# A batched matmul kernel on one core: one more turn, jumped over, at the front of TensorE's loop

## The chip, the cores and the metric

The kernel runs on one core of one Trainium2 chip. A core has five engines that each run their own list of instructions and meet through semaphores: TensorE (PE, matmuls), VectorE (DVE), ScalarE (ACT), GpSimd (POOL) and SyncE (SP, which here issues transfers only). Sixteen DMA engines move data between the chip's memory (HBM) and the core's on-chip memory. The metric is the device time of one execution in microseconds (us); lower is better.

## The reference

```python
x, y: float32 of shape (8, 12, 512, 64)
out = np.einsum('bhtc,bhsc->bhts', x, y)      # float32 of shape (8, 12, 512, 512)
```

There are 96 heads; each is a product of a 512x64 matrix with the transpose of another 512x64 matrix. The inputs have 25.17 MB together, the output has 100.66 MB.

## The kernel before

**Tiles.** The 96 heads are taken in 6 groups of 16. A group's x or y is one transfer of 2 MB (`load`, line 165), so there are 12 loads. An output tile is 2 MB too, and there are 48 of them. Five buffers of 2 MB, the `slots`, hold whatever comes in from HBM or goes out to it; loads and output tiles take them in turn.

**Stages.** ACT, DVE and POOL narrow a loaded slot to bf16 (`compress`), put x in an order fit for a transposition (`mix`), and DVE transposes 32x32 blocks (`transposes`, lines 214 and 223). PE multiplies (line 255, and line 262 for two tiles in each turn whose rows are laid out so that one store of 4 MB covers two tiles), writing into one of two PSUM buffers `pm0` and `pm1`, each half a tile. ACT copies a finished half from PSUM into a slot (`result`, line 409). SP stores the slot (`store`, lines 396 and 400). One output tile, number 41 (`SPLIT`), is made in two ways: half of its rows go the normal way, the other half are computed in five pieces late in the run (`pieces`, line 338), and sent by SP and POOL in small transfers (`send`, lines 373 and 382); POOL also issues two tiny reads (`step`, line 360).

**Order.** The whole work lies in one critical section in which the program writes the semaphore waits itself. A helper, `emit`, adds an instruction to an engine, works out which counts it has to wait for, and notes the count that the instruction will raise. All engines but PE are written out straight. PE alone runs a loop (`all_products`): 6 turns, 8 output tiles in a turn. Its waits compare a semaphore with a register: the counter `t` takes the values 8, 16, ... 48, and `counts` holds t-7 to t. Before tile j it waits until `tr` (transposes finished) has reached its count, at j = 0 and 4, and before each half tile until `ev0` or `ev1` (halves copied out of PSUM, plus one at the start) has reached `counts[j]`. So that PE's first half tile need not wait, ACT raises `ev0` and `ev1` by one at the start (line 431). Inside the loop stand jumps: at j = 1 and j = 5 one that skips the five late pieces in all turns but the last (line 286), and at the end of a turn two for its last two tiles (line 293), which are done in the narrow way in the first and the last turn and in the wide way in the others.

**The end.** When the critical section is over on all engines, a last store of 2 MB goes out (line 478), and the run ends when it has landed.

Of the kernel before, what the change touches and what calls it, by code (L numbers as in the profile page):

```python
# [9 lines left out]
def kernel(  # L10
# [22 lines left out]
    nc = tc.nc  # L33
# [8 lines left out]
    V = G // 4  # L42
    K = 8
    E = R // K
    D = 32
    SLOTS = 5
    TURNS = NH // 2
    SPLIT = V * NH - 2 * V + 1
    GROUP = 4
# [16 lines left out]
    wide = out.rearrange("b h t s -> (b h t s)").rearrange(  # L66
        "(o u g q n) -> o g q u n", u=2, g=V // 2, q=Q * E, n=2 * K * S
    )
# [3 lines left out]
    ps = ctx.enter_context(tc.tile_pool(name="ps", bufs=1, space=bass.MemoryType.PSUM))  # L72
    slot_row = sb.tile([P, SLOTS * K * S], fp32, name="slots")
    slots = [slot_row[:, i * K * S:(i + 1) * K * S] for i in range(SLOTS)]
    keep = sb.tile([P, (NG - 1) * R * D + (2 * NG - 1) * R // 2 * D], u32, name="keep")
# [16 lines left out]
    sems, ticks, known, snaps, writer, readers = {}, {}, {e: {} for e in engines}, {}, {}, {}  # L92
# [23 lines left out]
    def emit(name, make, reads=(), writes=(), dma=None, lane=None, known_by=None, held=None):  # L116

        points = [writer[r] for r in (*reads, *writes) if r in writer]
        points += [v for w in writes for v in readers.get(w, ())]
        if name == "pool" and name in ticks:  # L120
            points.append((name, ticks[name]))
        need(name, points, known_by, held)
        p, step = (lane or name, V if lane == "tr" else 1) if dma is None else (f"dma{dma}", 16)
        if p not in sems:
            sems[p] = tc.alloc_semaphore(p)
        if held is not None:
            held.append(make)
        elif make is not None:
            make().then_inc(sems[p], step)
        at = (p, ticks.get(p, 0) + step)  # L130
        ticks[p] = at[1]
        snaps[at] = {**known[name], p: at[1]}
        if dma is None:
            for q in lanes.get(name, (name,)):
                snaps[at][q] = ticks.get(q, 0)
        for r in reads:
            readers.setdefault(r, []).append(at)
        for w in writes:
            writer[w], readers[w] = at, []
# [17 lines left out]
    def slot():  # L157
        made_slots.append((len(made_slots) + 1) % SLOTS)
        return made_slots[-1]

    def load(n):
        i = loaded[n] = slot()
        emit(
            "sp",
            lambda: nc.sync.dma_start(slots[i], (yv if n % 2 else xv)[n // 2]),  # L165
            writes=both(i),
            dma=i,
        )
# [74 lines left out]
    def products(o, k):  # L243
        i, half, pm = o // V, o // V % 2, k // 4
        emit("pe", None, [("xT", half), ("yT", half)] + [("x_wide",)] * ((i + 1) * V - 1 in WIDE), [("pm", pm)],
             known_by=[(f"ev{pm}", o + 1), ("tr", (i + 1) * V)])

    def four(j, pm, wide):
        half, h = divmod(j, V)
        xT = xTs[half].bitcast(bf16).rearrange("p (k h m) -> p k h m", k=K, h=V)  # L250
        yT = yTs[half].bitcast(bf16)
        xw = ybs[1][0].bitcast(bf16).rearrange("p (k h w m) -> p k h w m", k=K, h=2, w=2)
        for b in range(4):
            if not wide:
                last = nc.tensor.matmul(  # L255
                    pms[pm][:, b, :], xT[:, 4 * pm + b, h, :], yT[:, h * S:(h + 1) * S],
                    start=True, stop=True,
                )
                continue
            for i in range(2):  # L260
                at = V - 2 + i
                last = nc.tensor.matmul(  # L262
                    pms[pm][i * 64:(i + 1) * 64, b, :], xw[:, 4 * pm + b, i, j % 2, :],
                    yT[:, at * S:(at + 1) * S],
                    start=True, stop=True,
                )
        return last

    def all_products():

        with nc.tensor.Fori(2 * V, 2 * V * TURNS + 1, 2 * V) as t:
            counts = [nc.tensor.snap(t - i) for i in range(2 * V - 1, 0, -1)] + [t]

            def tile(j, wide=False):

                if j % V == 0:
                    nc.tensor.wait_ge(sems["tr"], counts[j + V - 1])
                for pm in range(2):
                    nc.tensor.wait_ge(sems[f"ev{pm}"], counts[j])
                    four(j, pm, wide).then_inc(sems["pe"], 1)  # L280

            for j in range(2 * V - 2):
                tile(j)
                for o in BEHIND:
                    if o % (2 * V) == j:
                        with nc.tensor.If(t == 2 * V * (o // (2 * V) + 1)):
                            for step in held[o]:
                                if callable(step):
                                    step().then_inc(sems["pe"], 1)
                                else:  # L290
                                    nc.tensor.wait_ge(sems[step[0]], step[1])
            for wide, turns in enumerate((t % (2 * V * (TURNS - 1)) == 2 * V, t % (2 * V * (TURNS - 1)) != 2 * V)):
                with nc.tensor.If(turns):
                    for j in range(2 * V - 2, 2 * V):
                        tile(j, bool(wide))
# [59 lines left out]
    def step(at):  # L355

        to = spare[0:17:4, :, at * D // 2:(at + 1) * D // 2]
        emit(
            "pool",
            lambda: nc.gpsimd.dma_start(to, xv[0, 0:5].rearrange("p (a b c) -> p a b c", a=2, c=D)[:, :, 0, :D // 2]),  # L360
            dma="side",
        )
# [39 lines left out]
    def result(o, s):  # L402

        for k in range(0, K, 4):
            pm = k // 4
            products(o, k)
            emit(
                "act",
                lambda: nc.scalar.activation(  # L409
                    slots[s][:, k * S:(k + 4) * S], pms[pm].rearrange("p j s -> p (j s)"), COPY  # L410
                ),
                [("pm", pm)],
                [("slot", s, pm)],
                lane=f"ev{pm}",
            )
        if o < V * NH - 1:
            store(o, s)

    def prepare(i):

        if i < NH:
            transposes(i)
        if i + 1 < NH:
            for part in range(4):
                mix(i + 1, "dve", part)

    with tc.tile_critical(sync_engine=mybir.EngineType.Pool) as work:  # L427
        for at in range(2):
            sems[f"ev{at}"] = tc.alloc_semaphore(f"ev{at}")
            ticks[f"ev{at}"] = 1  # L430
            nc.scalar.sem_inc(sems[f"ev{at}"], 1)
        for g in range(SLOTS):
            load(g)
        step(0)
        for half, name in enumerate(("dve", "pool")):
            emit(
                name,
                lambda: engines[name].memset(xbs[half], 0.0),  # L438
                writes=[("xb", half, part) for part in range(4)],
            )  # L440
        front = []
        for n in range(2 * NG):
            if n == 11:
                result(3, slot())
            compress(n)
            mix(n // 4, "pool", n % 4)
            if n == 4:
                transposes(0)
            if n < 5:
                load(n + SLOTS)  # L450
            elif n in (6, 8):
                load(n // 2 + 7)
            elif n < 10:
                front.append(slot())
            if n > 7 and n < 11:
                result(n - 8, front[n - 8])
            if n == 9:
                transposes(1)
        prepare(2)
        for o in range(V, V * NH):  # L460
            result(o, slot())
            if o in BEHIND:
                pieces(o)
            if o == max(BEHIND):
                send()
            if o % V == V - 1:
                prepare(o // V + 2)
            if o == SPLIT - V - 1:
                pick()
        all_products()  # L470
    with tc.tile_critical() as rest:
        need("dve", [(p, ticks[p]) for p in ("dmaside", *(f"dma{i}" for i in range(SLOTS)))])
    tc.add_manual_dep(
# [40 lines left out]
```

## Time and profile before

| what | value |
|---|---|
| time, median of 3 runs | 299.59 us (299.47 to 299.66) |
| the profiled execution's own time | 299.59 us |
| its span, first to last instruction | 297.8 us |
| mean granted TensorE clock | 0.812 |
| bytes moved | 125.87 MB, mean 423 GB/s |
| busy: ACT, DVE, PE, POOL | 213.9, 161.9, 138.2, 58.5 us |
| last store issued | 287.17 us after the span's start |

The profile shows one execution. The span leaves out 1.79 us around the first and the last instruction (299.59 - 297.8). "DMA" in the profile's strip of forty slices is the busy share of the sixteen DMA engines. A transfer of 2 MB is cut into 128 packets of 16,384 bytes, eight for each DMA engine, and every DMA engine raises the transfer's semaphore by one when its own eight are done; the trace keeps these sixteen times for each transfer, so it shows by how much the slowest of the sixteen is behind the others. Packets of kind "instruction" carry program code to an engine, over the same DMA engines.

### The profile page before, as it was taken

The numbers are of one execution on the slowest core, as the hardware profiler recorded it, in microseconds if no ns is written. First come the engines' busy times: TensorE is split into PE (matmuls) and PEld (weight loads), VectorE is DVE, ScalarE is ACT, GpSimd is POOL, SyncE is SP. The second block draws the span as 40 slices with busy tenths as digits, with TensorE's granted clock in tenths as the row PEclk, the third lists the DMA queues.
The fourth block names the chain that finished last, engine by engine and source line by source line (L and its number), as shares of the span: only waits on it lengthen the run. The fifth ranks groups of instructions, "written<-read, shape, count | busy, mean of one in ns | idle before, by whom it ended". The sixth has DMA issues, their size and how long they took to land.

```text
span 297.8 us, 1449 instructions
## 1 busy us (share of the span) xinstructions
PE 138.2 (46%) x466; PEld 38.4 (13%) x466; DVE 161.9 (54%) x85; ACT 213.9 (72%) x111; POOL 58.5 (20%) x27
## 2 busy tenths in 40 slices
PE   0000040457655655743765844555827656755500
PEld 0000010111111111110121111211102112211100
DVE  2167797899929692935808639168095344103000
ACT  1665666999999987681998647978549965496900
POOL 3399999992000000000000000000000000002000
PEclk9999999998799997695598575996557986599755
DMA  7999999999999999999999999999999999999997
GB/s 275 429 429 436 427 429 425 429 427 434 434 425 431 434 431 424 436 447 416 427 438 428 453 414 429 429 431 429 429 436 429 423 425 462 394 434 431 423 407 319
DMA packets 8219, 125.87 MB, mean 423 GB/s; under 512 B 1036, under 2 KB 1036, under 8 KB 1052
## 3 DMA queue, kind: packets, MB, share of 16 engines
q1 hardware_dynamic: 8056, 125.11, 98.7%
q0 software_dynamic: 160, 0.72, 0.6%
q8 instruction: 1, 0.02, 0.0%
q14 instruction: 2, 0.02, 0.0%
HBM read 25.17 MB, written 100.66 MB: 423 GB/s over the span
## 4 chain that ended last, share of the span: by engine, by line
DMA 52%; ACT 29%; PE 6%; issue 4%; DVE 3%; ACTq 1%; SPq 0%; POOLq 0%
DMA out_dram<-slots 38%; ACT slots L409 26%; DMA slots<-in_y_dram 7%; DMA slots<-in_x_dram 6%; PE pm L255 4%; ACT keep L147 3%; DVE keep L149 3%; PE pm L338 2%; ACTq L427 1%; SPq L165 0%; ACTq L109 0%; SPq L109 0%; SPq L509 0%; POOLq L427 0%; POOLq L498 0%
## 5 line engine op out<-in xcount | busy, mean ns | idle before, releaser
L409 ACT ACTIVATE slots<-pm 128x2048 f32<-128x2048 f32 x96 | 173.4, 1892 | 43.1 <-DMA out_dram<-slots 33.9
L255 PE MATMUL pm<-yT,xT 128*128 128x512 bf16 x320 | 113.0, 498 | 125.1 <-ACT slots L409 83.4
L214 DVE STREAM_TRANSPOSE xT<-xb 128x2048 uint32<-128x2048 uint32 x12 | 46.7, 3889 | 66.7 <-PE pm L255 32.8
L255 PEld LDWEIGHTS pm<-yT,xT 128*128 128x128 bf16 x320 | 30.0, 114 | 208.2 <-ACT slots L409 132.6
L147 ACT ACTIVATE keep<-slots 128x4096 bf16<-128x4096 f32 (+1 forms) x12 | 36.5, 3042 | 21.5 <-DMA slots<-in_x_dram 16.3
L149 DVE COPY xb<-keep 32x2048 bf16<-32x2048 bf16 x36 | 47.0, 1306 | 1.0
L149 DVE CAST keep<-slots 64x2048 bf16<-64x2048 f32 x12 | 36.2, 3018 | 17.1 <-DMA slots<-in_y_dram 16.9
L373 POOL DMA_DIRECT2D out_dram<-keep x2 | 1.1, 564 | 205.0 <-ACT keep L147 205.0
L149 POOL COPY xb<-keep 32x2048 bf16<-32x2048 bf16 x12 | 36.3, 3024 | 9.2 <-ACT keep L147 8.4
L262 PE MATMUL pm<-yT,keep 128*64 128x512 bf16 x128 | 18.4, 415 | 12.4 <-ACT slots L409 12.4
L223 DVE STREAM_TRANSPOSE yT<-keep 128x1024 uint32<-128x1024 uint32 x12 | 23.1, 1926 | 0.0
L149 DVE COPY keep<-pm 96x2048 f32<-96x2048 f32 x3 | 6.9, 2287 | 24.9 <-PE pm L338 24.9
L149 POOL CAST keep<-slots 64x2048 bf16<-64x2048 f32 x6 | 17.8, 2970 | 1.4 <-DMA slots<-in_y_dram 0.8
L262 PEld LDWEIGHTS pm<-yT,keep 128*64 128x64 bf16 x128 | 6.2, 114 | 24.3 <-ACT slots L409 20.5
L338 PE MATMUL pm<-yT,keep 128*96 128x512 bf16 x18 | 6.9, 515 | 4.1 <-ACT slots L409 4.1
L147 ACT ACTIVATE keep<-pm 96x2048 f32<-96x2048 f32 (+1 forms) x2 | 2.9, 1446 | 2.8 <-PE pm L338 2.8
L338 PEld LDWEIGHTS pm<-yT,keep 128*96 128x96 bf16 x18 | 2.3, 151 | 8.3 <-issue 3.6
L234 DVE COPY keep<-xT 128x1024 uint32<-128x1024 uint32 x4 | 2.7, 674 | 0.0
L438 DVE MEMSET xb<- 128x2048 uint32 x1 | 1.8, 1765 | 1.4 <-PEq L498 1.4
L147 ACT ACT_TABLE_LOAD x1 | 1.3, 1283 | 1.0 <-PEq L498 1.0
L438 POOL MEMSET xb<- 128x2048 uint32 x1 | 1.8, 1823 | 0.0
L360 POOL DMA_DIRECT2D spare<-in_x_dram x2 | 1.2, 618 | 1.2 <-POOLq L427 1.2
(6 smaller groups left out, 1.4 us busy)
## 6 DMA issues: line engine op xcount, KB each, us to landing
out_dram<-slots SPq DMA_DIRECT2D x39, 2048.0 KB, 17.1
out_dram<-slots SPq DMA_DIRECT2D x4, 4096.0 KB, 20.8
slots<-in_x_dram SPq DMA_DIRECT2D x6, 2048.0 KB, 18.6
slots<-in_y_dram SPq DMA_DIRECT2D x6, 2048.0 KB, 20.8
out_dram<-slots SPq DMA_DIRECT2D x1, 1024.0 KB, 18.3
out_dram<-keep POOLq DMA_DIRECT2D x2, 352.0 KB, 10.0
out_dram<-keep SPq DMA_DIRECT2D x2, 128.0 KB
out_dram<-keep SPq DMA_DIRECT2D x1, 64.0 KB
```

Source lines behind the costliest of these rows:

```text
L147: lambda: nc.scalar.activation(dst, src, COPY)
L149: else engines[name].tensor_copy(dst, src),
L214: lambda: nc.vector.transpose(xTs[half].rearrange("p (k r e) -> p k e r", k=K, e=E), xbs[half].rearrange("p (k e c) -> p k e c", k=K, e=E),),
L223: lambda: nc.vector.transpose(yTs[half].rearrange("p (r j) -> p j r", r=D), ybs[half][b].rearrange("p (j c) -> p j c", c=D),),
L234: lambda: nc.vector.tensor_copy(x_wide, xTs[1].rearrange("p (k h q w) -> p k h w q", k=K, h=V, w=2)[:, :, V - 2:],),
L255: last = nc.tensor.matmul(pms[pm][:, b, :], xT[:, 4 * pm + b, h, :], yT[:, h * S:(h + 1) * S], start=True, stop=True,)
L262: last = nc.tensor.matmul(pms[pm][i * 64:(i + 1) * 64, b, :], xw[:, 4 * pm + b, i, j % 2, :], yT[:, at * S:(at + 1) * S], start=True, stop ...
L338: last = nc.tensor.matmul(pms[pm][:96, b, :], picked[:, bank, :], yT[:, h * S:(h + 1) * S], start=True, stop=True,)
L360: lambda: nc.gpsimd.dma_start(to, xv[0, 0:5].rearrange("p (a b c) -> p a b c", a=2, c=D)[:, :, 0, :D // 2]),
L409: lambda: nc.scalar.activation(slots[s][:, k * S:(k + 4) * S], pms[pm].rearrange("p j s -> p (j s)"), COPY),
L427: with tc.tile_critical(sync_engine=mybir.EngineType.Pool) as work:
L438: lambda: engines[name].memset(xbs[half], 0.0),
```

## The change

The loop starts at `t` = 8 still, but runs to 56: seven turns. In the first of them, an `If(t > TURN)` around the whole body sends PE past it, so that PE goes from the loop's head to its foot and back. The other six turns do the same work as before, with `t` from 16 to 56. As the registers are 8 higher, the semaphores are too: ACT raises `ev0` and `ev1` by 9 in place of 1, and `tr` by 8, at the start. The tests that pick the last turn, and the first and last, are moved by one turn.

```diff
+    TURN = 2 * V
...
     def products(o, k):
...
-             known_by=[(f"ev{pm}", o + 1), ("tr", (i + 1) * V)])
+             known_by=[(f"ev{pm}", TURN + o + 1), ("tr", TURN + (i + 1) * V)])
...
-        with nc.tensor.Fori(2 * V, 2 * V * TURNS + 1, 2 * V) as t:
+        with nc.tensor.Fori(TURN, TURN * (TURNS + 1) + 1, TURN) as t, nc.tensor.If(t > TURN):
             counts = [nc.tensor.snap(t - i) for i in range(2 * V - 1, 0, -1)] + [t]
...
-                        with nc.tensor.If(t == 2 * V * (o // (2 * V) + 1)):
+                        with nc.tensor.If(t == TURN * (o // TURN + 2)):
...
-            for wide, turns in enumerate((t % (2 * V * (TURNS - 1)) == 2 * V, t % (2 * V * (TURNS - 1)) != 2 * V)):
+            for wide, turns in enumerate((t % (TURN * (TURNS - 1)) == 2 * TURN, t % (TURN * (TURNS - 1)) != 2 * TURN)):
...
-        for at in range(2):
-            sems[f"ev{at}"] = tc.alloc_semaphore(f"ev{at}")
-            ticks[f"ev{at}"] = 1
-            nc.scalar.sem_inc(sems[f"ev{at}"], 1)
+        for lane, count in (("ev0", TURN + 1), ("ev1", TURN + 1), ("tr", TURN)):
+            sems[lane] = tc.alloc_semaphore(lane)
+            ticks[lane] = count
+            nc.scalar.sem_inc(sems[lane], count)
```

`V` is 4 and `TURNS` is 6, so `TURN` is 8 and a loop turn makes 8 output tiles.

## The prediction

> **What bounds the kernel now.** I read the page first: the engines' busy time, the strip of forty slices, and the DMA queues.
>
> ```profile
> PE 138.2 (46%) x466; PEld 38.4 (13%) x466; DVE 161.9 (54%) x85; ACT 213.9 (72%) x111; POOL 58.5 (20%) x27
> ...
> DMA  7999999999999999999999999999999999999997
> ...
> q1 hardware_dynamic: 8056, 125.11, 98.7%
> q0 software_dynamic: 160, 0.72, 0.6%
> q8 instruction: 1, 0.02, 0.0%
> q14 instruction: 2, 0.02, 0.0%
> ```
>
> No engine is busy for more than 72% of the span, while the sixteen DMA engines are busy in every slice: the only loss is in the first and the last. So PE, ACT and DVE matter only where they would let the DMA engines run dry, and the run ends when the slowest DMA engine has done its share. Three code fetches lie inside the span as well. The next question is where PE stands in time, from PE's waits and the timeline of PE and SP:
>
> ```profile
> PE pm L255 <- ACT slots L409: 83.4, 59, 12.7
> PE pm L255 <- DVE yT L223: 37.2, 1, 37.2
> ...
> 37.16 3.59 PE L255 MATMUL pm<-yT,xT 128*128 128x512 bf16 x8 [37.16 <-DVE yT L223]
> ...
> 87.79 1.04 PE L255 MATMUL pm<-yT,xT 128*128 128x512 bf16 x4 [0.73 <-ACT slots L409]
> ...
> 0.89 0.39 SPq L165 DMA_DIRECT2D slots<-in_x_dram  x1
> ```
>
> PE has nothing to do until 37.16 us, and from then on it mostly waits for ACT; 0.73 us before each half tile is typical. Third, the loop's own instructions, by source line (271 is the loop, 293 the end-of-turn tests, 431 ACT's raising of the counts):
>
> ```profile
> L271 PEldq COMPARE_BRANCH  x6: 67/208/221, 86.5 to 279.2; - x6
> ...
> L293 PEldq COMPARE_BRANCH  x12: 66/139/359, 79.0 to 278.8; - x12
> ...
> L431 ACTq EVENT_SEMAPHORE  x2: 17/17/17, 0.9 to 1.0; - x2
> ```
>
> A jump costs 66 to 359 ns. The 359 ns one stands at 86.03 us, the end of the first turn, where PE jumps over the wide tiles to the loop's foot for the first time; the same jump in the last turn takes 213 ns. The jump back takes 221 ns the first time, 207 or 208 ns later. Then the DMA view of the stretch from 89 to 92 us:
>
> ```profile
> q1 hardware_dynamic: 91, 1.25, 98.0%
> q8 instruction: 1, 0.02, 2.0%
> ```
>
> The trace puts this packet at 90.27 us: 16,384 bytes of code, 0.94 us long, the only one in queue q8. It comes 4.2 us after the first jump to the loop's foot and never again in five further turns. I infer that it is PE's: PE's first arrival in the last part of its code asks for the piece behind it. The two q14 packets (8,192 bytes, 116.3 and 162.0 us) go with no PE jump of their own that I can find.
>
> **What a code fetch costs.** Here the sixteen end times of each transfer decide. Up to the transfer whose ends lie about 85.96 us, the latest DMA engine is 0.58 us behind the median. In the next one, about 90.82 us, one engine that had been at +0.05 us is at +1.37 us: the fetch has cost that engine 1.32 us, and it stays so behind (1.35 us up to 193 us). A second engine falls behind by some 0.04 to 0.1 us with every store from about 72 us on, with no code packet near it, to 2.41 us in the store whose ends lie about 278.57 us. There the late ones are +2.41, +1.27, +0.33, +0.31 and +0.17 us. In the last store they are +0.59, +0.34, +0.33, +0.20 and some +0.06 us. A packet of 16,384 bytes takes 0.61 us, so this fits if the small transfers of `send` gave the slowest engine three packets fewer than the others (2.41 - 3 x 0.61 = 0.58) and the fetching one two fewer (1.27 - 2 x 0.61 = 0.05). The engine that ends the run is then the steadily falling one, not the one that fetched code.
>
> **The change, part by part.** *The empty turn.* One test, taken (0.07 to 0.36 us), the foot, one jump back (0.21 to 0.22 us): at most 0.6 us of PE from about 1.2 us on, inside its 37.16 us of waiting. Should code have to be fetched for it, 4.2 us (the delay seen at 86 us) twice still leaves more than 25 us. Cost 0. *The test in six real turns.* 6 x 0.07 = 0.4 us if not taken, 6 x 0.21 = 1.3 us if all were as dear as a taken one. Turn starts lie behind waits like the 0.73 us above, and behind PE stands ACT, which waits for landed stores for 33.9 us in all, and behind ACT the DMA queue, which never empties. Cost 0; without that cover, 0.4 to 1.3 us. *ACT's third increment.* 17 ns, some 0.07 us from one to the next, ahead of a table load that ends at 2.30 us while ACT's first copy starts at 8.86 us. Cost 0. *The higher counts* change no instruction, and every wait is released by the same event.
>
> *The fetch moves.* PE now reaches the foot at about 1.5 us. If my reading is right, the q8 packet goes from 90.27 us to the front: as early as 2.5 us by SP's first transfer (issued 0.89 us, first packet 1.91 us), as late as 5.7 us by the 4.2 us above. The data begin at 1.91 us, so it still falls on busy DMA engines. Its cost to the end has these bounds. Low: if the fetching engine is, against my arithmetic, the last one, and the fetch gets into idle time, the end comes when the next is done. The landings of the last store end with 296.475, 296.632, 296.634 and 296.878 us, so that is -0.244 us. High: the engine is late by a second fetch as well, +1.32 - (0.59 - 0.05) = +0.78 us. I take 0: with one fetch, early or late, the engine is at +0.05 us or earlier, and the one at +0.59 us decides. It is nearest to the row, since everything from 90 us on has already run with this lateness.
>
> *What is late next.* An engine late by 1.32 us from the start would make loads land up to 0.8 us later (1.37 - 0.58) between 8 and 90 us. The tightest place is the third store: issued at 68.54 us, first packets possible 1.02 us later at 69.56 us, while the earliest engine is free for it at 71.1 us or so (the store ahead of it ends on its engines from 71.11 us). 1.5 us of room against 0.8 us: no gap. The last store waits 7.4 us for POOL's end, which hangs on POOL's own transfers, and is issued at 287.17 us, while the store before it runs until 291.35 us on the earliest engine: room as well.
>
> **Sum.** 299.59 us for the profiled execution, equal to the median of the three runs, + 0 = 299.6 us.
>
> **A rule that speaks against it.** In the rows, one code packet in six turns and jumps back of 207 to 221 ns say that PE's loop stays in its memory. The Trainium skill ("Runtime: NRT & Kernel Launch", section "Instruction fetch mechanics") says that a taken branch whose target is outside the current two-page window forces a fetch before execution goes on. By that rule the long jump and the jump back could each fetch; the trace agrees only as far as one fetch after the first long jump.
>
> **Rivals.** *One fetch more (slower).* Place: the long jump over the whole body at 1.2 us, then back; the part of the code that PE leaves is not held, and is fetched again over the same DMA engine. Price: +1.32 us on that engine, 299.59 + 0.78 = 300.37 us; it decides as soon as the engine is later by over 0.54 us. Two more would give 301.7 us. For it: the first long jump did cost 146 ns more than later ones, and was followed by a fetch. Against it: five later pairs of jumps fetched nothing. *The fetching engine is the last (a little faster).* 299.59 - 0.24 = 299.35 us; for it, that it was 1.27 us late shortly before the end; against it, that the packet count explains the end to 0.02 us with the other engine. *The fetch does not move.* The q8 packet may hang on how far PE has run, not on the jump; then it stays at about 90 us and the time is 299.6 us. *The front starves (slower).* If the fetch among the first packets, which take up to 2.07 us each, cost 2.5 us instead of 1.32 us, loads would land 1.9 us late, the third store would leave a gap of 0.4 us on all engines: 300.0 us. *Much faster* has no mechanism: even with all four late engines cured, the twelve others end about 0.57 us earlier than the last, 0.19% of the time.
>
> **How the numbers follow.** 0.2% (0.6 us) is about what a measurement of this kernel can tell from no change. Chances: unchanged end with the fetch at the front 0.50; fetch not moved 0.12; a little faster 0.12 (all of these within 0.2%, range 299.2 to 299.9 us); a fetch more 0.16, of which nearly all beyond +0.6 us; the front starves 0.05, half of it beyond; something that no row here shows 0.05, on the fast side. With a part of the small cases spilling over: faster 0.07, same 0.74, slower 0.19. The range takes in -0.24 us with some margin and the single extra fetch: 299.2 to 300.5 us.
>
> **What would show it.** Right: the q8 packet lies within the first 6 us and no other follows; near 90 us no DMA engine falls back by 1.3 us; the 359 ns jump sits at the front; PE's first matmul starts at about 37.2 us (up to 0.8 us later); the last store's latest landing is about 0.6 us behind the median. Wrong: two or more q8 packets, one engine over 1.2 us behind at the end, a slice of the DMA strip under 9 near 70 us, or a last store issued well after 287.2 us.

## The result, and the profile after

The changed kernel takes 300.39 us (median of 8 runs, 300.23 to 300.85), the kernel before beside it 299.54 us (8 runs, 299.47 to 299.76). The ratio is 1.0029, with a 95% interval of 1.0020 to 1.0039: a small loss, but a clear one. The profiled execution took 300.23 us with a span of 298.4 us, so 0.6 us more than the profiled one before, in the span as in the time. It is the shortest of the eight, so the profile has 0.64 us of a loss that is 0.85 us by the medians.

The page of the changed kernel, its busy times, DMA strip and queues:

```profile
PE 133.0 (45%) x466; PEld 37.5 (13%) x466; DVE 161.8 (54%) x85; ACT 213.6 (72%) x111; POOL 58.5 (20%) x27
...
DMA  7999999999999999999999999999999999999997
...
q1 hardware_dynamic: 8056, 125.11, 98.8%
q0 software_dynamic: 160, 0.72, 0.6%
q8 instruction: 1, 0.02, 0.0%
q14 instruction: 2, 0.02, 0.0%
```

Nothing here points to a loss. The same packets, the same bytes, one q8 packet (the code packet of the prediction) as before, no slice of the strip under 9 but the first and the last, and no engine busier. The two views in which the prediction said what to look for come next. First the jumps by source line (272 is the loop with its new test, 294 the end-of-turn tests), and PE's first matmuls on its timeline:

```profile
L272 PEldq COMPARE_BRANCH  x14: 67/142/358, 1.2 to 279.1; - x14
...
L294 PEldq COMPARE_BRANCH  x12: 66/138/216, 80.0 to 278.8; - x12
...
38.13 2.31 PE L256 MATMUL pm<-yT,xT 128*128 128x512 bf16 x5 [38.13 <-DVE yT L224]
```

Line 272 now has 14 branches in seven turns, and the 358 ns one is among them: it is the jump over the body, at 1.24 us. PE's first matmul waits for DVE until 38.13 us, 0.97 us later than before. Second, the DMA queues from 3 to 8 us:

```profile
q1 hardware_dynamic: 127, 1.92, 90.8%
q8 instruction: 1, 0.02, 1.2%
q0 software_dynamic: 32, 0.00, 0.4%
```

and from 89 to 92 us, where the code packet was before:

```profile
q1 hardware_dynamic: 91, 1.25, 97.2%
```

The code packet has moved from 90.27 to 5.49 us, and no other came. So the change does what it says. The loss shows in a table by stretch. Its columns are the stretch and its length; the busy time of PE, PE's loads, DVE, ACT and POOL with their counts; the granted clock; the DMA share; and GB/s. The kernel before:

```profile
100.00:140.00 40.00, 22.27 (x84) 6.22 (x84) 24.98 (x14) 29.08 (x17) 0.00 (x0) 0.81 1.01 432
140.00:200.00 60.00, 35.31 (x136) 9.85 (x136) 33.99 (x21) 47.06 (x26) 0.00 (x0) 0.76 1.00 430
```

and after:

```profile
100.00:140.00 40.00, 21.89 (x86) 6.10 (x84) 25.62 (x14) 29.92 (x17) 0.00 (x0) 0.87 1.01 429
140.00:200.00 60.00, 34.42 (x135) 9.74 (x136) 32.95 (x20) 46.97 (x26) 0.00 (x0) 0.78 1.01 427
```

The DMA engines are fully busy in both, yet they move 0.7% less in the same time (429 against 432, 427 against 430). Each packet takes longer. The packets' own durations say it more sharply; these are means, in ns, over the packets of 16,384 bytes:

| stretch, us | before | after |
|---|---|---|
| 60 to 80 | 613.3 | 612.0 |
| 100 to 140 | 611.8 | 615.7 |
| 140 to 200 | 612.1 | 616.3 |
| 200 to 270 | 615.6 | 616.3 |

The means hide what a single packet does. While stores run undisturbed, nearly all of these packets take exactly 611 ns; the share that does so, in seven stretches:

| | 76 to 80 us | 80 to 84 | 92 to 96 | 100 to 104 | 112 to 116 | 188 to 196 | 228 to 236 |
|---|---|---|---|---|---|---|---|
| before | 0.94 | 0.97 | 0.93 | 0.94 | 0.97 | 0.87 | 0.37 |
| after | 0.93 | 0.89 | 0.81 | 0.61 | 0.31 | 0.33 | 0.35 |

Before, the longer packets come up from about 190 us on. After, they come up from 80 us on, step by step, and are the majority by 110 us. The sum fits: counting every packet as one of 16,384 bytes, 3.9 ns for each of the 65 that a DMA engine moves from 100 to 140 us (40 / 0.6157), 4.2 ns for 97 from 140 to 200 us and 0.7 ns for 114 from 200 to 270 us are 0.25 + 0.41 + 0.08 = 0.74 us. Summed over all packets as they are, the time per DMA engine rises from 296.01 to 296.81 us.

At the end of the run, the sixteen landings of the last store have their mean 0.88 us later (296.39, now 297.27), and the latest of them is less far behind it (0.49 us before, 0.25 us after), so the last landing moves by 0.64 us, from 296.878 to 297.517 us. That is the loss of the profiled execution.

What else happens at 80 us? SP's timeline has the fifth store's issue just there. Before:

```profile
78.60 4.39 SPq L400 DMA_DIRECT2D out_dram<-slots  x2
```

and after:

```profile
79.54 4.40 SPq L401 DMA_DIRECT2D out_dram<-slots  x2
```

The line joins two issues; the first, at its start, is the fifth store. The first DMA engine becomes free for it at 80.84 us before and at 80.75 us after, and the first load's first packet began 1.02 us after its issue (0.89 and 1.91 us). Reckoned with this, the store was ready 1.22 us ahead of need before, and 0.19 us ahead after. For a store even this is too much: in three runs below, engines did stand and wait for a store, four times in all, and its first packet came 1.20 us after its issue each time. With 1.20 us the store is ready 1.04 us ahead of need before, and 0.01 us ahead after, just in time. There is no gap: between 10 and 270 us no stretch shows idle DMA time that the kernel before does not show too.

### The profile page after: what moved, and what is told of

Read it like the earlier page. It is cut to its first block, busy times and chain, and to the rows that moved or that the text cites. A ratio compares the mean times of both kernels' runs of the same rounds, so it can differ in the third digit from the quotient of the medians.

```text
span 298.4 us, 1466 instructions
## 1 busy us (share of the span) xinstructions
PE 133.0 (45%) x466; PEld 37.5 (13%) x466; DVE 161.8 (54%) x85; ACT 213.6 (72%) x111; POOL 58.5 (20%) x27
## 4 chain that ended last, share of the span: by engine, by line
DMA 52%; ACT 28%; issue 5%; PE 5%; DVE 3%; ACTq 1%; SPq 0%; POOLq 0%
DMA out_dram<-slots 38%; ACT slots L410 26%; DMA slots<-in_y_dram 7%; DMA slots<-in_x_dram 6%; PE pm L256 4%; DVE keep L150 3%; ACT keep L148 3%; PE pm L339 1%; ACTq L428 1%; SPq L166 0%; ACTq L110 0%; SPq L110 0%; SPq L510 0%; POOLq L428 0%; POOLq L499 0%
## 5 line engine op out<-in xcount | busy, mean ns | idle before, releaser
L256 PE MATMUL pm<-yT,xT 128*128 128x512 bf16 x320 | 109.8, 486 | 130.7 <-ACT slots L410 88.0
L256 PEld LDWEIGHTS pm<-yT,xT 128*128 128x128 bf16 x320 | 29.4, 112 | 210.5 <-ACT slots L410 135.5
L263 PE MATMUL pm<-yT,keep 128*64 128x512 bf16 x128 | 16.9, 385 | 12.5 <-ACT slots L410 12.5
```

Of the source, the lines that this page charges most:

```text
L256: last = nc.tensor.matmul(pms[pm][:, b, :], xT[:, 4 * pm + b, h, :], yT[:, h * S:(h + 1) * S], start=True, stop=True,)
L263: last = nc.tensor.matmul(pms[pm][i * 64:(i + 1) * 64, b, :], xw[:, 4 * pm + b, i, j % 2, :], yT[:, at * S:(at + 1) * S], start=True, stop ...
```

## The experiments

The expectations name these theories. **A**: a DMA engine that is late from the start changes how the sixteen stand to each other, and this lengthens packets. **B**: the test in every turn, the counts or the semaphores cost something. **C**: the loads' landing late is the cost. **D**: as C, through one place only: ACT and SP come late, the fifth store is issued barely in time, and this starts the longer packets. **E**: as C, through ACT's lateness at all stores. **S**: an engine some 1.9 us behind the fastest in the stores' part lengthens packets by itself.

The numbers of all runs, in one table, to be read with the texts below. "Slack" is what the fifth store has between its issue + 1.02 us and the moment at which the first DMA engine is free for it; with the 1.20 us that stores showed, every figure of this column is 0.18 us smaller. "Spread" is the latest DMA engine against the earliest from 61 to 81 us. "Mean end" is that of the sixteen landings of the last store, "last" how far the latest is behind this mean.

| run | time, us | ratio (95%) | code packet at, us | slack, us | spread, us | packets 100 to 140, ns | 140 to 200, ns | mean end + last, us |
|---|---|---|---|---|---|---|---|---|
| before | 299.54 | | 90.27 | 1.22 | 0.84 | 611.8 | 612.1 | 296.39 + 0.49 |
| after | 300.39 | 1.0029 (1.0020 to 1.0039) | 5.49 | 0.19 | 1.91 | 615.7 | 616.3 | 297.27 + 0.25 |
| e1_no_turn | 299.54 | 1.0001 (0.9992 to 1.0010) | 90.19 | 1.37 | 0.71 | 611.8 | 611.9 | 296.22 + 0.48 |
| g1_test | 299.55 | 0.9998 (0.9989 to 1.0007) | 90.09 | 1.45 | 0.60 | 611.7 | 612.1 | 296.23 + 0.44 |
| e2_turn_at_37 | 300.44 | 1.0027 (1.0016 to 1.0039) | 40.63 | -0.01 | 2.30 | 617.0 | 616.2 | 297.58 + 0.37 |
| e3_pad190 | 299.79 | 1.0007 (0.9998 to 1.0016) | 58.65 | 1.27 | 1.87 | 611.8 | 612.0 | 296.39 + 0.62 |
| e4_read | 299.65 | 1.0004 (0.9995 to 1.0013) | 90.16 | 1.31 | 0.80 | 611.8 | 611.9 | 296.37 + 0.46 |
| e5_act_512 | 300.05 | 1.0013 (1.0004 to 1.0022) | 91.13 | 0.93 | 0.73 | 611.9 | 613.8 | 296.93 + 0.47 |
| e5_act_1024 | 300.56 | 1.0029 (1.0018 to 1.0041) | 91.33 | 0.20 | 0.79 | 615.7 | 616.3 | 297.33 + 0.55 |
| e5_act_2048 | 301.43 | 1.0062 (1.0046 to 1.0077) | 92.21 | -0.05 | 0.64 | 617.0 | 616.2 | 298.14 + 0.57 |
| f1_store5 | 300.96 | 1.0045 (1.0031 to 1.0059) | 90.59 | -0.15 | 0.61 | 617.0 | 616.3 | 297.77 + 0.57 |
| e6_relief | 300.29 | 1.0020 (1.0010 to 1.0029) | 5.46 | 1.05 | 2.2 | 611.8 | 614.8 | 296.81 + 0.82 |
| f2_relief_after | 300.24 | 1.0023 (1.0014 to 1.0032) | 5.57 | 1.35 | 1.92 | 611.9 | 613.9 | 296.69 + 0.80 |
| f3_relief_before | 299.49 | 0.9999 (0.9990 to 1.0008) | 89.23 | 2.29 | 0.85 | 611.7 | 611.9 | 296.23 + 0.72 |

**Everything but the empty turn.** The changed kernel, with the loop begun at its second turn:

```diff
-        with nc.tensor.Fori(TURN, TURN * (TURNS + 1) + 1, TURN) as t, nc.tensor.If(t > TURN):
+        with nc.tensor.Fori(2 * TURN, TURN * (TURNS + 1) + 1, TURN) as t, nc.tensor.If(t > TURN):
```

> The changed kernel without its empty turn: the loop starts at 16, so the counts, the order of the semaphores and the test around the body stay, and only the jump at the front goes. Theory A (the code fetch at the front makes one DMA engine late from the start, the sixteen engines stand otherwise to each other in time, and their packets take longer from about 86 us on instead of 193 us): the fetch is back at 86 to 91 us and the time is 299.4 to 299.7 us. Theory B (the test in each turn, the counts or the semaphores cost): 300.3 to 300.5 us.

It took 299.54 us, as before. But line 272 has only six branches in its trace:

```profile
L272 PEldq COMPARE_BRANCH  x6: 67/208/221, 86.4 to 278.4; - x6
```

These are the six at the loop's foot, five jumps back and a last one that falls through in 67 ns: a test that is always true by the loop's bounds was left out of the program. So this run keeps the higher counts and takes away the empty turn and the test together. A second kernel keeps a test that can't be decided beforehand, though it too is true in all six turns:

```diff
-        with nc.tensor.Fori(TURN, TURN * (TURNS + 1) + 1, TURN) as t, nc.tensor.If(t > TURN):
+        with nc.tensor.Fori(2 * TURN, TURN * (TURNS + 1) + 1, TURN) as t, nc.tensor.If(t % (3 * TURN) != 1):
```

> The changed kernel without its empty turn but with a test around the body in each of the six turns that is never true of any turn but has to be made (a remainder and a compare); all other instructions of the five engines are those of the changed kernel. Without the empty turn the code fetch is expected at 90 us again. Theory B (the test in each turn costs, and explains what is left of the loss when the fifth store is issued early enough): 300.2 to 300.4 us. If the fetch at the front is behind all of it: 299.4 to 299.7 us.

```profile
L272 PEldq COMPARE_BRANCH  x12: 67/76/227, 1.3 to 279.6; - x12
```

Now there are twelve: six tests that fall through, in 67 to 77 ns, and the six at the foot. The time is 299.55 us, the code packet is at 90.09 us, the packets stay short. The test, the counts and the third increment cost nothing that can be told (ratio 0.9989 to 1.0007); B falls. The whole loss comes with the empty turn.

**When the fetch comes.** The empty turn at 37 us in place of 1 us, just ahead of the first matmul, and so in the middle of the loads:

```diff
-        with nc.tensor.Fori(TURN, TURN * (TURNS + 1) + 1, TURN) as t, nc.tensor.If(t > TURN):
+        with nc.tensor.Fori(TURN, TURN * (TURNS + 1) + 1, TURN) as t, ExitStack() as body:
+            nc.tensor.wait_ge(sems["tr"], TURN + V)
+            body.enter_context(nc.tensor.If(t > TURN))
```

> The changed kernel with one wait more at the loop's head, for the first transposed y, so that PE takes the empty turn at about 37 us instead of 1.2 us, and the code packet comes at about 41 us, in the loads still but behind most of them. Theory A in its simple form (late before the stores begin is what costs): 300.2 to 300.6 us, packets of 615 ns and more from about 90 us on. Theory C (the first loads land up to 1 us later, and that delay is what costs): 299.5 us, as loads up to 41 us are on time. Theory B: 300.4 us.

The kernel before, with 190 increments of an unused semaphore ahead of PE's loop, which move all code behind them to a later place in PE's program:

```diff
+        pad = tc.alloc_semaphore("pad")
+        for _ in range(190):
+            nc.tensor.sem_inc(pad, 1)
```

> The kernel before with 190 increments of an unused semaphore on PE ahead of the loop, and no empty turn, no new test and no other counts: PE runs through them in its first 20 us and so reaches the later part of its code early. Theory A: a code packet somewhere in 5 to 25 us, one DMA engine late by 1.3 us from there on, no packet at 90 us, and 300.1 to 300.6 us. Theory B: 299.5 us, since nothing of the loop is changed.

Two more dates for the fetch were had. The DMA queues of the first from 39 to 42 us, where its code packet is:

```profile
q1 hardware_dynamic: 81, 1.23, 97.2%
q8 instruction: 1, 0.02, 2.2%
```

and of the second from 57 to 60 us:

```profile
q1 hardware_dynamic: 78, 1.26, 100.5%
q8 instruction: 1, 0.02, 2.2%
```

The second date was not the expected one (5 to 25 us), and it happened to be the more useful. The trace shows why it came then. In each of the fourteen kernels of the table one jump in PE's loop takes 355 to 360 ns, all others at most 231 ns, and the code packet begins 3.7 to 4.8 us after that one. Before, it is the jump to the loop's foot at 86.03 us; with the 190 increments it is the first jump over the five late pieces, at 54.98 us. So the packet is PE's, as the prediction inferred, and it follows a jump here too.

At 40.63 us the fetch still delays loads that ACT waits for, the fifth store is issued at 79.95 us with no slack left, and the run costs as much as the changed kernel. At 58.65 us the same fetch makes one DMA engine as late (spread 1.87 us against 1.91 us after), but behind the loads that count. The fifth store goes out as early as before:

```profile
78.55 4.40 SPq L403 DMA_DIRECT2D out_dram<-slots  x2
```

The stores' packets stay at 612 ns until about 190 us, and the time is 299.79 us, which can't be told from the kernel before (the 11 runs with the increments lie from 299.38 to 300.27 us, more widely than the others). A late engine in the stores' part is thus not enough to cause the loss; that speaks against A and S, and for something that reaches the stores through the loads.

**A late engine with no code.** The kernel before, with one small read of x into one partition at the start, meant to load one DMA engine only:

```diff
+        emit(
+            "act",
+            lambda: nc.scalar.dma_start(keep[0:1, 3 * R * D:5 * R * D].bitcast(fp32), xv[0, 0:1]),
+            writes=[("xk", 3), ("xk", 4)],
+            dma="extra",
+        )
```

> The kernel before with one read of 16,384 bytes in a single packet, issued by ACT on its own queue at the front, into a place that is overwritten later; the code fetch stays at 90 us. It makes one DMA engine late from the start, but maybe another one than the code packet does, and by 0.6 to 1.3 us. Theory A if any late engine will do: 300.0 to 300.6 us. Theory A if it has to be that engine, and theory B: 299.5 to 299.8 us.

It took 299.65 us, but its trace shows no clearly late DMA engine (up to 86 us the latest is 0.50 to 0.58 us behind the median, 0.58 to 0.69 us in the kernel before), so it says nothing on the theories.

**ACT late, with no fetch.** The kernel before, with one more copy of 512, 1024 or 2048 columns on ACT behind the ninth load's:

```diff
+            if n == 8:
+                copy("act", dst[:, :1024], slots[i][:, :1024], both(i), [("xk", xk)])
```

> The kernel before, in which ACT copies the first 512 columns of the fifth x a second time to the same place, at about 48 us, some 0.6 us of work where ACT has no idle time behind it until 78 us. The code fetch stays at 90 us and no DMA engine is made late. Theory D (late loads make ACT and SP late; in the changed kernel the fifth store is issued only 1.2 us before the first DMA engine is free for it, against 2.2 us before; from that store on packets get longer): fifth store issued at about 79.2 us, 1.6 us ahead; 299.5 to 300.0 us. Theory S (one engine 1.9 us behind the fastest during the stores is what lengthens packets): 299.5 us.

> The same with 1024 columns, some 1.05 us, which makes ACT as late as it is in the changed kernel, with all DMA engines on time. Theory D: fifth store issued at about 79.6 us, 1.2 us ahead or less, packets of 615 ns and more from about 86 us on, 300.2 to 300.5 us. Theory S: 299.5 us.

> The same with 2048 columns, some 1.9 us. The fifth store is issued about 0.3 us ahead of need, while the first packets take 1.0 us to come: all sixteen engines stand idle for 0.6 to 0.8 us. Theory D: that idle time and the longer packets, 300.6 to 301.2 us. Theory S: the idle time alone, 300.1 to 300.4 us.

The middle one is the changed kernel's double without a fetch at the front and without a late engine (spread 0.79 us). Its fifth store, and its table by stretch:

```profile
79.61 4.39 SPq L402 DMA_DIRECT2D out_dram<-slots  x2
```

```profile
100.00:140.00 40.00, 22.49 (x87) 6.17 (x84) 24.72 (x14) 29.99 (x17) 0.00 (x0) 0.82 1.00 428
140.00:200.00 60.00, 35.83 (x135) 9.97 (x136) 34.16 (x20) 46.97 (x26) 0.00 (x0) 0.76 1.01 428
```

Its fifth store is issued at 79.61 us (after: 79.54 us) with 0.20 us of slack (0.19 us); its packets take 615.7 and 616.3 ns (the same), and the ratio is the same, 1.0029. With half the delay the slack is 0.93 us, the packets lengthen only from about 156 us on, and the loss is 1.0013. With twice the delay there are gaps, 7.0 engine-us from 70 to 85 us or 0.44 us for each of the sixteen, on top of the longer packets: 1.0062. The loss can be had in full with no DMA engine late, so lateness on ACT and SP is sufficient, and A is not needed for it. D forecast the order of the three runs, and less than each measured: 300.05, 300.56 and 301.43 us lie 0.05, 0.06 and 0.23 us above its ranges.

**The fifth store alone.** The kernel before, with SP holding the fifth store for a step of DVE's; ACT stays on time:

```diff
+        if o == V:
+            need("sp", [("dve", ticks["dve"] - 1)])
```

> The kernel before, in which SP alone is held back at one place: the fifth store also waits for VectorE's third reordering copy, which ends at about 80.0 us, so it is issued at 80.0 us instead of 78.6 us, 0.8 us ahead of the first free DMA engine. ACT, PE and the code fetch stay where they were, and no DMA engine is late. Theory D (the late issue of this store alone turns the packets from 611.6 to about 615.8 ns): the idle time of 0.2 to 0.4 us and the longer packets, 300.3 to 300.9 us. Theory E (it is ACT's lateness as a whole, at all stores from 48 us on): the idle time alone, 299.6 to 299.9 us.

```profile
80.09 2.68 SPq L402 DMA_DIRECT2D out_dram<-slots  x2
```

```profile
100.00:140.00 40.00, 23.28 (x84) 6.47 (x84) 24.03 (x14) 28.88 (x16) 0.00 (x0) 0.77 1.00 427
140.00:200.00 60.00, 32.55 (x136) 9.48 (x136) 34.35 (x20) 46.97 (x26) 0.00 (x0) 0.81 1.01 428
```

The store comes 1.5 us late, the fault of one issue, and leaves a gap of 2.23 engine-us from 80 to 85 us, 0.14 us for each DMA engine. The run loses 1.4 us (300.96 us). Nine tenths of that is not the gap: the share of packets at 611 ns falls at once (0.95 from 76 to 80 us, 0.40 from 80 to 84 us, where the changed kernel takes 30 us for it), and their mean behind it is 616 to 617 ns until the end, 427 and 428 GB/s in place of 432 and 430 in the two stretches shown. One issue is enough for the longer packets, with ACT on time; that is D, against E. The store came later against need than planned, though (0.8 us ahead was expected), and the gap does something that the changed kernel doesn't show: the sixteen engines end the fourth store 0.61 us apart and the fifth 0.20 us apart. So this run shows that one late store suffices, and not what one does that comes just in time.

**The slack given back.** The changed kernel, in which one copy of ACT's at the tenth load is cut short, so that ACT catches up. The first kernel, with `R // 4` in place of the `2` below, leaves out half of that copy, the second nearly all of it:

```diff
+                some = 2 if n == 9 and (half, ch) == (1, 1) else R // 2
...
-                    yv2[ch * 64:(ch + 1) * 64],
+                    yv2[ch * 64:(ch + 1) * 64, :some],
...
-                    ),
+                    )[:, :some],
...
+        emit("pool", lambda: nc.gpsimd.memset(ybs[1][4][64:], 0), writes=[("yb", 1, 4, 1)])
```

> The changed kernel, in which ACT narrows only the first half of its quarter of the fifth y (2.48 us become about 1.3 us, at about 56 us); the other half is set to zero at the start, so some of the output is left out. The code fetch stays at the front and its DMA engine stays late; ACT and SP gain some 1.2 us before the fifth store. Theory D: fifth store issued at about 78.4 us, 2.3 us ahead, packets of 612 ns until about 190 us, 299.4 to 299.8 us. Theory S: 300.3 to 300.5 us.

> The changed kernel, in which ACT narrows only a sixteenth of its quarter of the fifth y (2.48 us become about 0.4 us); the rest is set to zero at the start, so some of the output is left out. The code fetch stays at the front with its late engine, while the fifth store is issued some 3 us ahead. Theory D: packets of 612 ns until about 190 us; left is only what the late engine itself adds at the end, 299.5 to 300.0 us. Theory S (the late engine by itself lengthens packets): longer packets from about 140 us on as with the smaller relief, 300.2 to 300.4 us.

and the second edit on the kernel before:

> The kernel before with the same relief of ACT (the same part of the output is left out), fetch at 90 us, no late engine until then, fifth store issued some 4 us ahead. If 2.2 us ahead was already enough: 299.4 to 299.6 us, packets longer from about 195 us on as in the kernel before. If more room is worth more: the longer packets come later, 299.0 to 299.3 us.

The second on the changed kernel:

```profile
78.61 4.40 SPq L402 DMA_DIRECT2D out_dram<-slots  x2
```

```profile
100.00:140.00 40.00, 24.62 (x84) 6.69 (x84) 24.53 (x14) 29.41 (x17) 0.00 (x0) 0.74 1.00 430
140.00:200.00 60.00, 32.89 (x136) 9.44 (x136) 34.36 (x20) 46.97 (x26) 0.00 (x0) 0.80 1.00 428
```

The fifth store is back at 78.61 us, and with it the short packets: 611.9 ns from 100 to 140 us, where the changed kernel had 615.7 ns. But they last only until about 145 us (0.65 of them at 611 ns from 148 to 156 us, before 0.94), and the time is 300.24 us (300.29 us with the smaller relief): only 0.10 to 0.15 us better than the changed kernel, with intervals that overlap. The table's last column says where the rest is. Of the 0.61 us by which the last landing is later than before, 0.30 us is the mean end (packet time per DMA engine 296.22 us against 296.01 us), and 0.31 us the latest DMA engine's distance from that mean, 0.80 us in place of 0.49 us. The changed kernel has 0.88 us and -0.24 us there. On the kernel before, the same relief gives 299.49 us: more slack than 1.2 us brings nothing, and the relief itself does no harm. D's forecasts for the two reliefs of the changed kernel, 299.4 to 299.8 and 299.5 to 300.0 us, both failed.

So D is shown for the onset at 80 us, by the copies on ACT and by the reliefs, and a late store is sufficient for a loss of this size. It isn't the whole of the loss, and taking it away gives back only a small part. S had the right times for the two reliefs, 300.2 to 300.4 us, yet the same spread begun at 58.65 us cost nothing that can be told.

**Open.** Two things. Why packets get longer after a store that is issued barely in time, with no DMA engine idle, no run shows; the traces give only the fact. That the engines come to stand closer together, as behind the gap above, is not the reason in every run: with the second relief the twelve earliest ends of a store lie 0.49 us apart at 139 and at 154 us and 0.82 us at 228 us, while the share of packets at 611 ns there is 0.94, 0.67 and 0.39. And with the slack restored, the fetch at the front still costs some 0.7 us, half through an earlier onset (140 us), half through the end of the run being less even. What starts that onset, and whether it is a DMA engine's lateness at the change from loads to stores, no run shows: it needs a kernel in which one engine is late by 1.6 us from the front and all loads land on time. The unevenness at the end also varies among undisturbed runs, 0.44 to 0.72 us, so part of that half may be chance of the profiled execution. No kernel here beats the one before; those that match it lie from 299.49 to 299.79 us.

## Why the prediction was right, and where it was not

The time lies in the range (299.2 to 300.5 us) but not at the forecast: 299.6 us was said, 300.39 us came, and the side that came, slower by over 0.2%, had 0.19. That the range holds it is luck: its upper end came from the price of a second fetch, and there was none. Nor did any of the signs named for a wrong forecast appear: one q8 packet, no slice of the strip under 9 near 70 us, no engine 1.2 us behind at the end, and a last store issued early, at 285.97 us. They looked for gaps and late engines, and the time went into packets.

- **The empty turn and the test, cost 0: right.** The jump over the body took 358 ns at 1.24 us, the jump back 227 ns, later tests 77 ns, all inside PE's waiting; the kernel with the test but no empty turn took 299.55 us.
- **The fetch moves to 2.5 to 5.7 us, and no second follows: right.** One q8 packet, at 5.49 us. Near 90 us no DMA engine falls back. The rule of the Trainium skill weighed there ("Runtime: NRT & Kernel Launch", section "Instruction fetch mechanics") is that a taken branch out of the current two-page window fetches before execution goes on. The trace shows no such stop: PE took the jump back at 1.76 us and the next test at 2.22 us, while the packet began at 5.49 us, and of the loop's fourteen branches one was followed by a fetch. Which of the jumps leave such a window no run shows.
- **The engine's lateness, 1.32 us: somewhat too small.** It is 1.44 us behind the median in the first load, and 1.58 to 1.59 us from 27 to 81 us.
- **Loads land up to 0.8 us later: nearly.** It was 0.97 us at PE's first matmul, and 0.94 us at SP's fifth store.
- **The tightest place: wrong.** The third store was named, with 1.5 us of room. It had that, and kept 0.50 us of it (its issue is 1.52 us ahead of the first free DMA engine). But the fifth store had only 1.22 us before, and kept 0.19 us. The traces of before held this number; the search stopped at the third. The 1.02 us from issue to first packet, too, was the first load's; for the stores it was 1.20 us.
- **"Room against lateness: no gap", so cost 0: this is the step that failed.** There was indeed no gap. The step put at nothing what a store that is barely in time does to the packets behind it: they take +0.74 us in sum between 100 and 270 us, with full DMA engines throughout, and the kernel before has the same packets and the same loss when ACT alone is late. It is not all: with the slack given back, 0.10 to 0.15 us of the 0.85 us came back, and what the rest hangs on stays open. The reason given for the 0, "everything from 90 us on has already run with this lateness", failed with it: before, the engine became late only when eight stores had been issued, the last two of them 3.5 us and more ahead of need.
- **Which engine ends the run: not shown.** The trace doesn't name the DMA engines. In the stores up to 275 us they can be followed by their order, and there the one that fetched falls back from 1.59 us to about 0.25 us behind the median, if it is the one that another engine overtakes at about 150 us; the small transfers then mix the order. What is seen is that the latest of the last store is closer to the others, 0.26 us behind the median in place of 0.56 us. This gain is of the size of the 0.24 us that the rival "the fetching engine is the last" had as its ceiling, but it is outweighed by a mean end that is 0.88 us later.
- **The rivals.** "One fetch more" gave 300.37 us, which is almost the time measured, by a mechanism that did not occur. "The front starves" had the right chain, late loads and then late stores, with chance 0.05; its price was reckoned from a gap of DMA time at the third store, and needed 1.9 us of lateness where 0.97 us was enough.

## What to carry to other kernels

In a kernel whose DMA engines are always busy, a full strip does not say that nothing was lost: compare GB/s by stretch, or packet durations, at equal DMA share (here 432 and 429 GB/s at 1.01 from 100 to 140 us). List the slack of every store against the first free DMA engine, not only that of the one that looks tightest. Here 0.93 us of it already went with a loss of 0.13%, and 0.20 us with 0.29%, so such a slack was a price and not a cover. A code fetch took its time from one DMA engine among sixteen (1.32 us in the kernel before), and a transfer lands when its last engine has done its share; so the fetch cost most where a load was being waited for (300.39 and 300.44 us with the packet at 5.49 and 40.63 us), and nothing that can be told behind the loads (299.79 us at 58.65 us).

## What the runs showed of the hardware that was not expected

- The stores' packets of 16,384 bytes have two regimes with all DMA engines busy: 611 ns for about 95% of them, or a mean of 615 to 617 ns with only 0.2 to 0.45 of them at 611 ns. Every kernel here gets to the second at some point, and no run showed a lasting way back. By the slack of the table, 0.93 us at the fifth store put the onset at about 156 us, 0.20 us and less at 80 us; with 1.2 us and more, and no engine late from the front, it lay between 190 and 220 us. Where the third store had 0.21 us of slack (`e2_turn_at_37`) or left a gap (`e5_act_2048`), the onset was there, at 72 us; 0.50 us at the third store, in the changed kernel, started nothing yet (0.90 and 0.93 of the packets at 611 ns from 72 to 76 and from 76 to 80 us).
- One store held back until it left a gap of 0.14 us on each DMA engine cost 1.4 us of run time.
- From a store's issue to its first packet on an engine that stood waiting it took 1.20 us, in each of the four cases in the runs: `f1_store5`, `e2_turn_at_37`, and twice in `e5_act_2048`. The first load took 1.02 us.
- In every run exactly one PE jump took 355 to 360 ns, and the one code packet of queue q8 began 3.7 to 4.8 us after it. The delay is about the same with an idle PE at the front as in the middle of the run: 1.24 to 5.49 us, and 86.03 to 90.27 us. PE ran on in the meantime.
- Which jump that is depends on the code's position: 190 small instructions ahead of the loop moved the fetch from 90.27 to 58.65 us, with no jump added, and the long jump from the loop's foot at 86.03 us to the late pieces at 54.98 us.
